# Building the expert-gate matrix from bf16 one-hots of eight tokens at a time instead of fp32 one-hots of four

## The chip, the cores and the metric

The kernel runs on one core of one Trainium2 chip. The metric is the device time of one execution in microseconds (us). The median of three runs of the kernel before is 3040.92 us (3037.68 to 3048.45). The engines are named as in the profile: PE is TensorE's matrix multiply and PEld its weight load, DVE is VectorE, ACT is ScalarE, POOL is GpSimd, SP is SyncE, which issues most DMA transfers.

## The reference

The program computes two transformer blocks over 512 tokens of 1024 features. The change sits in the last part, a PEER layer: each token picks 16 experts out of 16384 (= 128 x 128) for each of 8 heads, so 128 slots per token, each with an expert number (i, j) and a gate.

```python
best_s, best_c = lax.top_k(cand.reshape(T, PEER_HEADS, PEER_TOPK * PEER_TOPK), PEER_TOPK)
gates = jax.nn.softmax(best_s, axis=-1)
...
u = jnp.take(expert_u, ib, axis=0)
act = jax.nn.gelu(jnp.einsum('td,thkd->thk', xb, u).astype(jnp.float32))
w = (gb * act).astype(xb.dtype)
v = jnp.take(expert_v, ib, axis=0)
return jnp.einsum('thk,thkd->td', w, v)
```

## The kernel before

The last 128 tokens gather their experts' rows by indirect DMA (`gather_rows`). The first 384 tokens (NDENSE = 3 blocks of 128) do it densely: for every j of 128 the kernel multiplies all 384 tokens with the 128 experts (i, j) on TensorE (`expert_act`, L1397 to L1407: 24 matmuls of 384 columns), multiplies the result with the gates of (i, j) for each token (`expert_gate`), and multiplies that with the experts' output rows (`expert_out`).

For that the gates must stand in a dense matrix: for each token a 128 x 128 matrix over (i, j) that is zero except at its 128 slots. `gate_matrix` makes it. The slots of a token lie on the 128 partitions; `slots_T` has put i, j and the gate there with three transposes. For a token, a one-hot row of i for each slot, scaled with the slot's gate, and a one-hot row of j for each slot are built; their product on TensorE, summed over the slots, is the token's matrix. Both factors are fp32, and TensorE runs an fp32 product as two instructions.

The work goes in groups of four tokens, 96 groups in all. The letters of GATED say how a group is built. In an "A" group VectorE compares an iota row with i and with j in one instruction (L1382, 1024 elements), and ScalarE scales the one-hot of i with the gate, one instruction a token (L1384). In a "D" group VectorE compares j for four tokens (L1386, 512 elements) and builds the scaled one-hot of i itself, one instruction a token (L1388). TensorE makes the four products (L1391) into a PSUM tile `pg` of two buffers, and ScalarE copies it out into the staging tile `gstage` (L1393). Every 8 groups the staging tile of 2 MB goes to HBM as `gd` (L1395); it is read back later as `gread`.

`peer` (from L1430) sets the order: 15 expert products stand beside the retrieval, 4 after it, and then 21 (j from 19 to 39) are laid among the groups. Expert product j waits in the program's order for a group some 10 back (NLAG), and the last three (NLATE) follow the last group. A planner then orders each engine's instructions by a simulated timeline, with the groups at high priority; each engine runs its own list strictly in that order. For every expert product a weight tile of 512 KB is loaded and split into a high part by ScalarE (L245) and a low part by GpSimd (L248). After the groups comes the dense loop over 128 j.

The buffers are set by one line, `P.open(eg, "gate", "gstage 2; ohA 4; ohB 3")`: tile name and count. A new tile of a name waits until every reader of the tile that held its place is done.

Of the kernel before, what the change touches and what calls it, by code (L numbers as in the profile page):

```python
# [11 lines left out]
BF16 = mybir.dt.bfloat16  # L12
U32 = mybir.dt.uint32
AF = mybir.ActivationFunctionType
ALU = mybir.AluOpType
# [29 lines left out]
NDENSE = 3  # L45
NFIFO = 40
IN_ORDER = ((0, 0), (0, 1), (0, 2), (0, 3), (1, 0), (1, 1), (1, 2), (1, 3))
GATED = "ADADADAD"
NBESIDE = 15
NEARLY, NLATE, NLAG = 19, 3, 10  # L50
GATE_AHEAD = 8
# [118 lines left out]
class Prog:  # L170
# [1189 lines left out]
    def slots_T(self, i):  # L1360

        nc = self.nc
        p = self.b("pslT", [128, 3, 128])
        for w, a in enumerate((*self.sel, self.gate)):
            nc.tensor.transpose(p[:, w, :], a[:, i].rearrange("p a b -> p (a b)"), self.ident)
        t_ = self.B([128, 3, 128], f"slT{i}", 1)
        nc.scalar.activation(t_, p, AF.Copy)
        return t_

    def gate_matrix(self, slT, gd):  # L1370

        nc = self.nc
        for b in range(NDENSE * 4):
            st = self.b("gstage", [128, 128, 32])
            for q in range(8):
                p = self.b("pg", [128, 4, 128])
                t_ = b * 32 + q * 4
                sl, k = slT[t_ // 128], t_ % 128
                A4, one = self.b("ohA", [128, 4, 128]), self.b("ohB", [128, 2, 4, 128])
                iota = lambda n: self.iota[:, None, None, :].to_broadcast([128, n, 4, 128])  # L1380
                if GATED[q] == "A":
                    nc.vector.tensor_tensor(one, iota(2), sl[:, 0:2, k:k + 4, None].to_broadcast([128, 2, 4, 128]), op=ALU.is_equal)  # L1382
                    for r in range(4):
                        nc.scalar.activation(A4[:, r], one[:, 0, r], AF.Copy, scale=sl[:, 2, k + r:k + r + 1])  # L1384
                else:
                    nc.vector.tensor_tensor(one[:, 1:2], iota(1), sl[:, 1:2, k:k + 4, None].to_broadcast([128, 1, 4, 128]), op=ALU.is_equal)  # L1386
                    for r in range(4):
                        nc.vector.tensor_scalar(A4[:, r], self.iota, sl[:, 0, k + r:k + r + 1], sl[:, 2, k + r:k + r + 1],  # L1388
                                                op0=ALU.is_equal, op1=ALU.mult)
                for r in range(4):  # L1390
                    last = nc.tensor.matmul(p[:, r, :], A4[:, r], one[:, 1, r], start=True, stop=True)  # L1391
                self.gates_done.append(last.ins)
                nc.scalar.activation(st[:, :, q * 4:q * 4 + 4], p.rearrange("p t j -> p j t"), AF.Copy)  # L1393
                yield
            nc.sync.dma_start(gd[b], st.rearrange("p j t -> p (j t)"))  # L1395
# [141 lines left out]
def body(tc, I, out, dbg=None, manual=False):  # L1537
    nc = tc.nc
    with ExitStack() as es:
        if manual:  # L1540
            es.enter_context(tc.manual_schedule())
        P = Prog(tc, es, I, dbg)
# [83 lines left out]
        with ExitStack() as e1:  # L1626
# [5 lines left out]
            a = P.hgrn_in(0, U)  # L1632
            for h in range(8):
                b = P.hgrn_in(h + 1, U) if h < 7 else None
# [3 lines left out]
                a = b  # L1638
# [26 lines left out]
        eg = ExitStack()  # L1665

        def open_q2():
            eq1.close()
            P.open(eg, "gate", "gstage 2; ohA 4; ohB 3")

        def open_v():
            eg.close()
            P.qp = P.open(es, "peer2", "none 1")
        P.open_q2, P.open_v = open_q2, open_v
        P.peer(H4, gd, xd, row, out)

# [15 lines left out]
```

## Time and profile before

| | |
|---|---|
| median of 3 runs | 3040.92 us |
| profiled execution: its own time | 3040.9 us |
| span of its instructions | 3039.1 us |
| PE busy | 2938.0 us (97%), 15129 matmuls |
| DVE busy | 1867.7 us (61%) |
| ACT busy | 1245.4 us (41%) |
| POOL busy | 1352.4 us (44%) |
| mean granted TensorE clock | 0.989 of full speed |
| DMA over the span | 155 GB/s |

Busy time counts instructions from start to end. Matmuls overlap in TensorE's pipeline, so the distance between two starts, not their duration, says what one costs. The busy share over the whole span is a mean over stages with different limits; the groups' stage is some 180 us of it, from 1940 to 2120 us.

### The profile page before, as it was taken

Reading aid. Unit: us, or ns where it says so; the run is one execution under the profiler, and the core shown is the slowest. Engines: PE = TensorE matmul, PEld = TensorE weight load, DVE = VectorE, ACT = ScalarE, POOL = GpSimd, SP = SyncE. Lnnn points to the kernel's source line nnn. Section 1 sums busy time; section 2 is a strip of 40 time slices with the busy share of each in tenths; the row PEclk is TensorE's granted clock in tenths of the full one; section 3 lists DMA queues with packets and bytes.
Section 4 is the critical chain, followed back from the end, with each engine's and each line's share of the span. In section 5 each row is a group of like instructions: output and inputs, shape, how many; then the busy total and the mean of one; then the engine's idle time right before and its main releaser. Section 6 shows DMA issues by size and latency. Waiting matters only on the chain.

```text
span 3039.1 us, 40262 instructions
## 1 busy us (share of the span) xinstructions
PE 2938.0 (97%) x15129; PEld 2540.3 (84%) x15129; DVE 1867.7 (61%) x3017; ACT 1245.4 (41%) x2120; POOL 1352.4 (44%) x926
## 2 busy tenths in 40 slices
PE   7998998999999999999999999989999999999998
PEld 6877787888878887888888888888899999999887
DVE  4237664444133663355532489898678877777898
ACT  5455654222232453244432344576333333333333
POOL 3223213222234662233332344422677777777765
PEclk9998999999999999999999999999999999999999
DMA  4220003333332212322233432355988888898987
GB/s 155 63 63 15 1 30 103 97 97 97 97 107 88 63 46 73 108 83 81 82 105 114 130 97 88 125 190 195 303 299 296 311 312 302 289 324 300 320 321 264
DMA packets 174355, 473.60 MB, mean 156 GB/s; under 512 B 15057, under 2 KB 64593, under 8 KB 172625
## 3 DMA queue, kind: packets, MB, share of 16 engines
q1 hardware_dynamic: 137296, 336.80, 34.0%
q0 software_dynamic: 36864, 134.23, 12.5%
q8 instruction: 119, 1.95, 0.3%
q14 instruction: 76, 0.61, 0.1%
HBM read 439.49 MB, written 31.46 MB: 155 GB/s over the span
## 4 chain that ended last, share of the span: by engine, by line
PE 78%; issue 6%; DVE 5%; DMA 5%; ACT 3%; POOL 3%; SPq 0%; POOLq 0%; DVEq 0%; ACTq 0%
PE acc L271 15%; PE acc L272 15%; PE acc L273 15%; DMA urow<-ev,ei 3%; PE A L273 3%; PE A L272 3%; PE A L271 3%; PE B L272 3%; PE B L271 3%; PE B L273 3%; PE pg L1391 2%; PE i L810 2%; POOL urow L1339 1%; DMA rawx<-ev 1%; PE lev L987 1%
## 5 line engine op out<-in xcount | busy, mean ns | idle before, releaser
L248 POOL TENSOR_TENSOR lo<-raw,hi 128x1024 fp32r<-128x1024 f32 x224 | 558.1, 2493 | 946.3 <-ACT hi L245 920.5
L271 PE MATMUL acc<-u,hi 128*128 128x512 f32 (+3 forms) x2344 | 857.6, 367 | 4.0 <-DVE sil L912 1.5
L272 PE MATMUL acc<-u,hi 128*128 128x512 f32 (+3 forms) x2344 | 856.8, 366 | 0.2 <-DVE u L477 0.2
L273 PE MATMUL acc<-u,lo 128*128 128x512 f32 (+3 forms) x2344 | 856.9, 366 | 0.0
L245 ACT ACTIVATE hi<-raw 128x1024 fp32r<-128x1024 f32 x447 | 472.3, 1057 | 901.2 <-PE acc L272 457.4
L248 DVE TENSOR_TENSOR lo<-raw,hi 128x1024 fp32r<-128x1024 f32 x223 | 316.1, 1417 | 297.3 <-ACT hi L245 297.0
L271 PEld LDWEIGHTS acc<-u,hi 128*128 128x128 f32 (+1 forms) x2344 | 443.8, 190 | 59.0 <-issue 2.7
L272 PEld LDWEIGHTS acc<-u,hi 128*128 128x128 f32 (+1 forms) x2344 | 444.1, 189 | 54.7 <-issue 2.7
L273 PEld LDWEIGHTS acc<-u,lo 128*128 128x128 f32 (+1 forms) x2344 | 444.0, 189 | 48.7 <-issue 0.6
L1347 DVE SCALAR_TENSOR_TENSOR urow<-urow,h4row 128x1024 f32<-128x1024 f32 x128 | 200.8, 1575 | 94.5 <-DMA urow<-eu,ei 94.3
L1357 DVE SCALAR_TENSOR_TENSOR po<-urow,act,po 128x1024 f32<-128x1024 f32 x127 | 188.9, 1487 | 66.3 <-DMA urow<-ev,ei 65.4
L1339 POOL DMA_INDIRECT urow<-eu,ei x128 | 188.4, 1472 | 32.9 <-issue 21.4
L1417 ACT ACTIVATE wh<-wf 128x384 fp32r<-128x384 f32 x128 | 67.2, 526 | 312.4 <-PE D L272 246.4
L1339 POOL DMA_INDIRECT urow<-ev,ei x128 | 171.2, 1337 | 43.8 <-DVE po L1357 18.0
L248 POOL TENSOR_TENSOR lox<-rawx,hix 128x1024 fp32r<-128x1024 f32 x53 | 134.8, 2543 | 92.7 <-ACT hix L245 92.5
L1391 PE MATMUL pg<-ohB,ohA 128*128 128x128 f32 x768 | 105.1, 286 | 19.0 <-ACT gstage L1393 17.1
L1391 PEld LDWEIGHTS pg<-ohB,ohA 128*128 128x128 f32 x768 | 98.7, 197 | 24.4 <-ACT gstage L1393 20.9
L1418 DVE TENSOR_TENSOR wl<-wf,wh 128x384 fp32r<-128x384 f32 x128 | 98.8, 773 | 6.8 <-ACT wh L1417 5.1
L1384 ACT ACTIVATE ohA<-ohB,slT 128x128 f32<-128x128 f32 x192 | 61.4, 392 | 41.8 <-DVE ohB L1382 41.7
L1414 DVE TENSOR_TENSOR wf<-eact,gread 128x384 f32<-128x384 f32 x98 | 67.0, 684 | 17.0 <-DMA gread<-gd 15.9
L1388 DVE TENSOR_SCALAR ohA<-iota,slT 128x128 f32<-128x128 f32 x192 | 76.6, 461 | 0.0
L245 ACT ACTIVATE hix<-rawx 128x1024 fp32r<-128x1024 f32 x53 | 55.7, 1052 | 27.4 <-DMA rawx<-ev 27.4
(574 smaller groups left out, 5511.1 us busy)
## 6 DMA issues: line engine op xcount, KB each, us to landing
raw<-ut SPq DMA_DIRECT2D x128, 512.0 KB
raw<-ev SPq DMA_DIRECT2D x75, 512.0 KB
rawx<-ev SPq DMA_DIRECT2D x53, 512.0 KB
raw<-w_ret SPq DMA_DIRECT2D x48, 512.0 KB
gd<-gstage SPq DMA_DIRECT2D x12, 2048.0 KB
gread<-gd SPq DMA_DIRECT2D x32, 768.0 KB
raw<-w_gu SPq DMA_DIRECT2D x44, 512.0 KB
raw<-w_hg SPq DMA_DIRECT2D x32, 512.0 KB
```

Of the source, the lines that this page charges most:

```text
L245: self.nc.scalar.activation(hi, raw, AF.Copy)
L248: r = eng.tensor_tensor(lo, raw, hi.bitcast(F32), op=ALU.subtract)
L271: mm(out, a[0], b[0], start=start, stop=False)
L272: mm(out, a[0], b[1], start=False, stop=False)
L273: return mm(out, a[1], b[0], start=False, stop=stop).ins
L1339: r = nc.gpsimd.indirect_dma_start(out=u, out_offset=None, in_=src, in_offset=bass.IndirectOffsetOnAxis(ap=ei[:, s:s + 1], axis=0))
L1347: nc.vector.scalar_tensor_tensor(u, u, 1.0, row, op0=ALU.mult, op1=ALU.mult, accum_out=act[:, s:s + 1])
L1357: nc.vector.scalar_tensor_tensor(o, u, act[:, s:s + 1], o, op0=ALU.mult, op1=ALU.add)
L1388: nc.vector.tensor_scalar(A4[:, r], self.iota, sl[:, 0, k + r:k + r + 1], sl[:, 2, k + r:k + r + 1], op0=ALU.is_equal, op1=ALU.mult)
L1391: last = nc.tensor.matmul(p[:, r, :], A4[:, r], one[:, 1, r], start=True, stop=True)
L1417: nc.scalar.activation(wh, wf, AF.Copy)
L1418: nc.vector.tensor_tensor(wl, wf, wh.bitcast(F32), op=ALU.subtract)
```

## The change

The one-hots become bf16. VectorE builds both one-hots of eight tokens (two groups, called an octet below) in one comparison of 16 x 128 elements. To let it read 16-bit elements two by two, every i and j is first written twice side by side (`ij`), and the views are cut into pairs.

The gates stay exact: each fp32 gate is split into three bf16 parts that add up to it (`g3`, three ScalarE copies and two VectorE subtractions for 128 tokens). In two octets of three VectorE multiplies the one-hot of j with each of the three parts (three instructions of 8 x 128 elements), and TensorE makes each token's matrix with three bf16 products summed in PSUM. In every third octet ScalarE brings both one-hots back to fp32, group by group (one copy, four scaled copies), and TensorE multiplies in fp32 as before.

The PSUM tiles alternate between the names `psc` and `pg`, two buffers each, so four in place of two. `slots_T` writes i and j as bf16 and the gates as fp32 with two copies. The one-hot buffers are two of each name, each now holding an octet (or, for the fp32 operands, a group).

```diff
-GATED = "ADADADAD"
...
     def gate_matrix(self, slT, gd):
...
+        io = self.b("iotab", [128, 128], BF16)
+        nc.vector.tensor_copy(io, self.iota)
+        pairs = lambda a: a.rearrange("p n (c e) -> p n c e", e=2)
         for b in range(NDENSE * 4):
             st = self.b("gstage", [128, 128, 32])
+            if b % 4 == 0:
+
+                ij, g3 = self.b("ij", [128, 16, 2, 8, 2], BF16), self.b("g3", [128, 3, 128, 2], BF16)
+                ij_, g = slT[b // 4]
+                for w in range(2):
+                    nc.scalar.activation(ij[:, :, w], ij_[:, w].rearrange("p (n r) -> p n r", r=8)[:, :, :, None].to_broadcast([128, 16, 8, 2]), AF.Copy)
+                rest, r_ = self.b("grest", [128, 128]), g
+                for w in range(3):
+                    nc.scalar.activation(g3[:, w], r_[:, :, None].to_broadcast([128, 128, 2]), AF.Copy)
+                    if w < 2:
+                        nc.vector.tensor_tensor(rest, r_, g3[:, w, :, 0], op=ALU.subtract)
+                        r_ = rest
             for q in range(8):
...
-                if GATED[q] == "A":
-                    nc.vector.tensor_tensor(one, iota(2), sl[:, 0:2, k:k + 4, None].to_broadcast([128, 2, 4, 128]), op=ALU.is_equal)
+                k = b % 4 * 32 + q * 4
+                fp32 = (b * 4 + q // 2) % 3 == 2
+                if q % 2 == 0:
+                    one = self.b("ohA", [128, 16, 128], BF16)
+                    nc.vector.tensor_tensor(pairs(one), pairs(io[:, None, :].to_broadcast([128, 16, 128])),
+                                            ij[:, k // 8].rearrange("p w r e -> p (w r) e")[:, :, None, :].to_broadcast([128, 16, 64, 2]),
+                                            op=ALU.is_equal)
+                    if not fp32:
+                        gb = self.b("ohB", [128, 3, 8, 128], BF16)
+                        for w in range(3):
+                            nc.vector.tensor_tensor(pairs(gb[:, w]), pairs(one[:, 8:16]),
+                                                    g3[:, w, k:k + 8, None, :].to_broadcast([128, 8, 64, 2]), op=ALU.mult)
+                p = self.b("pg" if q % 2 else "psc", [128, 4, 128])
+                o = q % 2 * 4
+                if fp32:
+                    gb = self.b("ohB", [128, 2, 4, 128])
+                    nc.scalar.activation(gb[:, 0], one[:, o:o + 4], AF.Copy)
                     for r in range(4):
-                        nc.scalar.activation(A4[:, r], one[:, 0, r], AF.Copy, scale=sl[:, 2, k + r:k + r + 1])
+                        nc.scalar.activation(gb[:, 1, r], one[:, 8 + o + r], AF.Copy, scale=g[:, k + r:k + r + 1])
+                    for r in range(4):
+                        last = nc.tensor.matmul(p[:, r, :], gb[:, 0, r], gb[:, 1, r], start=True, stop=True)
                 else:
-                    nc.vector.tensor_tensor(one[:, 1:2], iota(1), sl[:, 1:2, k:k + 4, None].to_broadcast([128, 1, 4, 128]), op=ALU.is_equal)
                     for r in range(4):
-                        nc.vector.tensor_scalar(A4[:, r], self.iota, sl[:, 0, k + r:k + r + 1], sl[:, 2, k + r:k + r + 1],
-                                                op0=ALU.is_equal, op1=ALU.mult)
-                for r in range(4):
-                    last = nc.tensor.matmul(p[:, r, :], A4[:, r], one[:, 1, r], start=True, stop=True)
+                        for w in range(3):
+                            last = nc.tensor.matmul(p[:, r, :], one[:, o + r], gb[:, w, o + r], start=w == 0, stop=w == 2)
...
-            P.open(eg, "gate", "gstage 2; ohA 4; ohB 3")
+            P.open(eg, "gate", "gstage 2; iotab 1; ij 1; g3 1; grest 1; ohA 2; ohB 2")
```

## Rows read from the trace of the kernel before

**Rows 1.** Instructions of L1391, the groups' products: ns min/median/max, first and last start.

```profile
L1391 PE MATMUL pg<-ohB,ohA x768: 271/275/481, 1941.6 to 2119.8; 128*128 128x128 f32 x192
```

**Rows 2.** Busy time by stretch: us, then the engines, clock, DMA share, GB/s.

```profile
1940.00:2120.00 180.00, 160.89 (x1132) 155.48 (x1133) 165.65 (x285) 129.07 (x319) 40.24 (x16) 0.98 0.48 176
2200.00:2800.00 600.00, 600.00 (x3035) 546.40 (x3034) 469.23 (x510) 213.12 (x291) 437.19 (x249) 1.00 0.88 305
2860.00:3020.00 160.00, 158.43 (x701) 130.60 (x700) 150.81 (x140) 56.61 (x76) 112.44 (x64) 1.00 0.91 325
```

**Rows 3.** Groups of instructions by line, 1941 to 2121 us: count, busy us, mean ns, idle.

```profile
L1388 DVE TENSOR_SCALAR ohA<-iota,slT 128x128 f32<-128x128 f32 x192 | 76.6, 461 | 0.0
L1384 ACT ACTIVATE ohA<-ohB,slT 128x128 f32<-128x128 f32 x192 | 61.4, 392 | 41.8 <-DVE ohB L1382 41.7
L1382 DVE TENSOR_TENSOR ohB<-iota,slT 128x1024 f32<-128x1024 f32 x46 | 56.1, 1219 | 6.9 <-PE pg L1391 6.5
L1393 ACT ACTIVATE gstage<-pg 128x512 f32<-128x512 f32 x96 | 53.6, 585 | 8.6 <-PE pg L1391 8.2
L1386 DVE TENSOR_TENSOR ohB<-iota,slT 128x512 f32<-128x512 f32 x47 | 43.1, 917 | 6.1 <-ACT ohA L1384 3.6 <-PE pg L1391 1.2 <-issue 1.2
L271 PE MATMUL acc<-u,hi 128*128 128x384 f32 x123 | 43.1, 350 | 0.0
L248 POOL TENSOR_TENSOR lo<-raw,hi 128x1024 fp32r<-128x1024 f32 x16 | 40.8, 2552 | 125.2 <-ACT hi L245 125.2
L245 ACT ACTIVATE hi<-raw 128x1024 fp32r<-128x1024 f32 x15 | 15.8, 1053 | 0.0
```

**Rows 4.** Waits from 1936 to 2122 us: total us, times, longest.

```profile
ACT ohA L1384 <- DVE ohB L1382: 41.7, 28, 2.8
...
PE pg L1391 <- ACT gstage L1393: 17.1, 16, 1.8
```

**Rows 5.** Timeline of VectorE with GpSimd idle: start us, us, instruction.

```profile
2113.01 1.22 DVE L1382 TENSOR_TENSOR ohB<-iota,slT 128x1024 f32<-128x1024 f32 x1
2114.14 0.69 DVE L1386 TENSOR_TENSOR ohB<-iota,slT 128x512 f32<-128x512 f32 x1
2114.75 1.11 DVE L1388 TENSOR_SCALAR ohA<-iota,slT 128x128 f32<-128x128 f32 x4
2115.77 1.22 DVE L1382 TENSOR_TENSOR ohB<-iota,slT 128x1024 f32<-128x1024 f32 x1
```

**Rows 6.** Timeline of GpSimd and VectorE around one weight split.

```profile
1967.16 2.88 POOL L248 TENSOR_TENSOR lo<-raw,hi 128x1024 fp32r<-128x1024 f32 x1 [8.12 <-ACT hi L245]
...
1967.71 2.87 DVE L1386 TENSOR_TENSOR ohB<-iota,slT 128x512 f32<-128x512 f32 x1
```

**Rows 7.** Timeline of PE: two groups' products; two expert matmuls, twelve apart.

```profile
2099.17 1.95 PE L1391 MATMUL pg<-ohB,ohA 128*128 128x128 f32 x16
...
2126.16 0.34 PE L271 MATMUL acc<-u,hi 128*128 128x384 f32 x1
...
2128.24 0.34 PE L271 MATMUL acc<-u,hi 128*128 128x384 f32 x1
```

**Rows 8.** Timeline of PE: 128-column matmuls of one instruction each (retention layer).

```profile
1509.37 0.27 PE L271 MATMUL s<-qk 128*128 128x128 f32 x1
1509.49 0.27 PE L272 MATMUL s<-qk 128*128 128x128 f32 x1
1509.60 0.28 PE L273 MATMUL s<-qk 128*128 128x128 f32 x1
```

**Rows 9.** Weight loads: of those matmuls, and the program's only bf16 ones.

```profile
L271 PEld LDWEIGHTS s<-qk x32: 187/188/193, 1266.6 to 1509.3; 128*128 128x128 f32 x32
...
L620 PEld LDWEIGHTS <-identb x32: 95/96/151, 66.4 to 181.3; 128*128 128x128 bf16 x32
```

**Rows 10.** ScalarE copies from SBUF of 512 and 256 elements, elsewhere in the program.

```profile
L322 ACT ACTIVATE qk<-ra 128x512 fp32r<-128x512 f32 x16 | 10.0, 628 | 10.8 <-POOL ra L1099 10.4
...
L886 ACT ACTIVATE lnsq<-lnd 128x256 f32<-128x256 f32 x8 | 3.3, 411 | 1.8 <-DVE lnd L884 1.8
```

More of the change, by code (lines that the diff above doesn't have):

```diff
@@ L1365, in slots_T @@
             nc.tensor.transpose(p[:, w, :], a[:, i].rearrange("p a b -> p (a b)"), self.ident)
-        t_ = self.B([128, 3, 128], f"slT{i}", 1)
-        nc.scalar.activation(t_, p, AF.Copy)
-        return t_
+        ij, g = self.B([128, 2, 128], f"ijT{i}", 1, BF16), self.B([128, 128], f"gT{i}", 1)
+        nc.scalar.activation(ij, p[:, 0:2], AF.Copy)
+        nc.scalar.activation(g, p[:, 2], AF.Copy)
+        return ij, g
     def gate_matrix(self, slT, gd):
         nc = self.nc
+        io = self.b("iotab", [128, 128], BF16)
@@ L1373, in gate_matrix @@
+        nc.vector.tensor_copy(io, self.iota)
+        pairs = lambda a: a.rearrange("p n (c e) -> p n c e", e=2)
         for b in range(NDENSE * 4):
             st = self.b("gstage", [128, 128, 32])
-            for q in range(8):
[L1376 to L1380, printed above, removed]
-                if GATED[q] == "A":
-                    nc.vector.tensor_tensor(one, iota(2), sl[:, 0:2, k:k + 4, None].to_broadcast([128, 2, 4, 128]), op=ALU.is_equal)
+            if b % 4 == 0:
[9 more added lines that the diff above has]
+                        r_ = rest
+            for q in range(8):
+                k = b % 4 * 32 + q * 4
[15 more added lines that the diff above has]
+                    nc.scalar.activation(gb[:, 0], one[:, o:o + 4], AF.Copy)
```

## The prediction

> **What bounds the kernel now.** I first placed the groups' stage: its products run from 1941.6 to 2119.8 us [rows 1]. Next I compared the stretches [rows 2]. From 2200 to 2800 us PE is busy all 600 us, and from 2860 to 3020 us 158.43 of 160, so the dense loop behind the stage runs at TensorE's pace and starts when the stage ends. In the stage DMA is busy 0.48, in the loop 0.88; the loop's loads start with the loop and move with it. So I count a microsecond won or lost in the stage as one at the end. The profiled execution took 3040.9 us beside a span of 3039.1, equal to the median of the runs, 3040.92; sums below are made against it.
>
> Inside the stage the fullest engine is VectorE: 165.65 us busy of 180 [rows 2]. Its own work is less. With GpSimd idle, one period of two groups steps from 2113.01 to 2114.14 (1.13 us for the comparison of 1024 elements), to 2114.75 (0.61 for that of 512), to 2115.77 (1.02 for four scaled one-hots): 2.76 us [rows 5], times 48 periods 132.5 us. Where a weight split runs on GpSimd, VectorE's instruction lasts with it: the 512-element comparison took 2.87 us in place of 0.69 beside a split of 2.88 [rows 5, 6]. There are 16 splits of 2.55 us [rows 3], 40.8 us, and 165.65 less 132.5 says that some 33 us of them fell on VectorE. The other 14 of the 180 us it waits. TensorE needs less: two groups' 16 instructions take 1.95 us less a last one of 0.28, over 15 steps, 0.11 us each [rows 1, 7], so 768 make 85.5 us; the expert matmuls step by 2.08/12 = 0.173 us [rows 7], and some 367 of them (123 from one of three lines [rows 3]) make 63.5: 149 of 180. ScalarE is busy 129 us [rows 2], and it is often early: it waits 41.7 us for VectorE's comparisons [rows 4].
>
> **The change, part by part.** *VectorE.* The new comparison covers 2048 bf16 elements an octet. If two 16-bit elements pass per step, that is the 1024 steps of the old one, 1.13 us; a multiplication of 1024 bf16 elements is 512 steps, 0.605 us [rows 5]. 48 x 1.13 + 32 x 3 x 0.605 = 54.4 + 58.1 = 112.5 us in place of 132.5: 20 us less. If each element takes a step, the slope of those two rows (0.52 us for 512 elements) makes 2.17 and 1.13 us, 104 + 108 = 212 us. No bf16 instruction with two tensors ran before, so both ends stay. I take the first: both operands and the output are 16-bit and laid in pairs.
> [...]
>
> *GpSimd's splits* are untouched, 33 us of VectorE. All new VectorE instructions have two SBUF tensors, like the one held up in [rows 6], so I keep 33.
>
> *TensorE.* A third of the groups stays fp32: 32 x 8 x 0.11 = 28.5 us. The other 64 have 12 bf16 products each, 768 in place of 512 instructions. By the expert matmuls 128 columns stream in 0.173/3 = 0.058 us [rows 7]. But single 128-column matmuls with 4-byte weights step by 0.11 us [rows 8], twice that, so there the weight load sets the pace. The bf16 loads last 96 ns where the others last 188 [rows 9], about half. So 0.058 us is the low end and 0.11 the high; by the load's ratio I take 0.06: 46 us. The stage's sum is 46 + 28.5 + 63.5 = 138 us. At 0.11 it is 84.5 + 28.5 + 63.5 = 176.5.
> [...]
>
> *ScalarE* loses 192 scaled copies (61.4 us) and gains 128 of 0.392 (50.2), 32 copies of 512 elements at 0.628 (20.1) and 15 small ones that prepare pairs and parts at 0.41 (6.2) [rows 3, 10]: 129 + 15 = 144 us. The 96 copies out of PSUM stay.
>
> *Starts and end.* For each 128 tokens `ij` and `g3` have one buffer, and three copies with two subtractions between make a chain of about 2 us (an estimate: three times 0.41 [rows 10] and two short subtractions) before VectorE can multiply. The comparison beside it hides about half of the three: 4 us, plus 2 at the first for the pair copies of 0.41 each [rows 10] and the cast. The last octet is fp32 and ends with ScalarE's two groups, 2 x 1.8 us, where the old one ended with VectorE: 3 us. Together 9 (bounds 4 and 15). No DMA is added or moved past another queue; the 12 writes of `gd` come at the stage's pace.
>
> *Waits.* The 17.1 us that TensorE waits for ScalarE's copies out of `pg` [rows 4] should nearly go with four PSUM tiles. What is late next is the one-hot buffer. An fp32 octet takes both places of `ohB`, and the next octet's multiplications wait until its first group has been copied by ScalarE (0.628 + 0.392 + three further ones at some 0.3, about 1.8 us), then multiplied, PE ending some 0.3 behind. So per three octets the chain is comparison 1.13, fp32 group 2.1, multiplications 1.82, comparison 1.13, multiplications 1.82: 8.0 us where VectorE's own work is 3 x 1.13 + 6 x 0.605 = 7.0. That is 1 us of wait in each of 16 cycles, 16 us, and it replaces the present 14. Behind the waiting multiplication stand VectorE's next comparison and with it all engines. If no wait shows, 0; if ScalarE's PSUM copies (0.585) and weight rounding (1.053) [rows 3] also stand ahead of each fp32 group, and expert matmuls ahead of its products, up to 2 us a cycle, 32.
>
> Sum for the 180 us: 112.5 + 33 + 9 + 16 = 170.5, 9.5 us less, 3040.9 - 9.5 = **3031 us**. With waits of 0 and starts of 4 it is 149.5, 3010; with 32 and 15 it is 192.5, 3053.
>
> **Rivals.** *The buffers eat the gain.* VectorE's 20 us are given back as waits for ScalarE and TensorE, which now stand in a two-place loop with it. For it: all three would be at 138 to 146 us of work (VectorE 112.5 + 33), close together, in strict order. Against it: ScalarE today waits more than it is waited for [rows 4]. It turns to a loss when waits and starts exceed 34.5 us. With 32 + 9 it gives 186.5: 3047 us.
> *TensorE becomes the bound, the side of a loss.* If a bf16 product costs 0.11 us, 176.5 us of products plus the 14 us of unfilled time of today make 190: 3051 us. It decides from about 0.10 us a product. Speaking for it is [rows 8], against it [rows 9]. [...]
> *VectorE does not read pairs.* 212 + 33 + 9 + some 6 of waits = 260 us: 3121 us. The pairs are then worthless. Against it is only the layout; nothing in the trace shows it.
>
> **How the numbers follow.** A run of this kernel tells about 0.3%, 9 us, from no change. The forecast case (pairs read, a light product, waits of 0 to 20 us, 3010 to 3036) has 0.50; of it 0.43 lies more than 9 us below and 0.07 within. The buffers have 0.27 (3036 to 3053): 0.16 within 9 us, 0.11 slower. TensorE as the bound has 0.13: 0.03 within, 0.10 slower. One element a step has 0.10, all slower. So faster 0.43, same 0.26, slower 0.31. The range 3010 to 3062 leaves out the last case alone, its high end some way above the 3051 of the second-last; the forecast's own range is 3010 to 3036.
>
> **What would show it.** In the changed profile: the comparison of 2048 elements at about 1.2 us and the multiplications at about 0.69 (2.2 and 1.2 if no pairs are read); bf16 products that step by about 0.06 us; TensorE's wait for the copies out of PSUM nearly gone; VectorE waiting for TensorE ahead of the multiplication behind each fp32 octet, about 1 us a cycle; the last product near 2110 us; and the loop's pace of 3035 matmuls in 600 us [rows 2] unchanged, so that the end moves by as much as the stage does. Wrong would make it: a planner's order that puts expert matmuls in front of groups that are ready, bf16 instructions that GpSimd holds up longer than before, or a loop whose start waits for a late `gread`.

## The result and the profile after

The changed kernel takes 3064.95 us (median of 4 runs, 3064.63 to 3072.39), the kernel before beside it 3041.9 us: a ratio of 1.008, 95% interval 1.0056 to 1.0104. It is slower by 0.8%; the forecast was 3031 us, range 3010 to 3062.

Nearly all of it lies in the groups' stage. The instructions of the groups' products in the changed kernel (ns min/median/max, first and last start):

```profile
L1416 PE MATMUL psc<-ohB,ohA x384: 216/219/330, 1941.2 to 2136.5; 128*128 128x128 bf16 x192
...
L1412 PE MATMUL pg<-ohB x128: 272/275/582, 1950.1 to 2141.8; 128*128 128x128 f32 x128
```

They run from 1941.2 to 2141.8 us, 200.6 us where the kernel before had 178.2 [rows 1]. That is 22.4 us of the 24.1 by which the span grew (3063.2 and 3039.1). Busy time by stretch, with the columns of [rows 2], shows the same from both sides:

```profile
1940.00:2140.00 200.00, 163.47 (x1376) 152.07 (x1375) 142.57 (x149) 129.21 (x293) 39.42 (x15) 0.89 0.41 158
2200.00:2800.00 600.00, 600.00 (x3034) 546.15 (x3033) 464.19 (x516) 211.76 (x289) 437.74 (x249) 1.00 0.87 305
```

The dense loop runs as before, 3034 matmuls in 600 us. In the stage VectorE is busy 142.57 us where it was 165.65, so its work did shrink, by 23 us. But it idles 57.4 of 200 us (200 - 142.57) where it idled 14.35 of 180. TensorE's granted clock in the stage fell from 0.98 to 0.89 of full speed. The groups of instructions (count, busy us, mean ns, idle ahead and what ended it):

```profile
L1402 DVE TENSOR_TENSOR ohB<-ohA,g 128x1024 bf16<-128x1024 bf16 x96 | 78.1, 869 | 13.7 <-PE psc L1412 6.4 <-PE pg L1412 3.4 <-PE pg L1416 1.8
L1396 DVE TENSOR_TENSOR ohA<-iotab,ij 128x2048 bf16<-128x2048 bf16 x48 | 65.9, 1376 | 45.9 <-PE pg L1416 27.5 <-ACT ij L1384 8.8 <-ACT ohB L1410 8.2
```

In [rows 3] VectorE idled 6.9 and 6.1 us ahead of its comparisons. Now it idles 45.9 us there, 27.5 of them until TensorE is done with products of `pg`, which are the last readers of an octet's place of `ohA`, and 8.2 until ScalarE has copied from such a place. And the waits of the stage (total us, times, longest) show that TensorE waits for VectorE in turn, while its old wait for the copies out of PSUM, 17.1 us in [rows 4], is down to 1.3:

```profile
PE psc L1416 <- DVE ohB L1402: 30.1, 29, 4.1
...
DVE ohA L1396 <- PE pg L1416: 27.5, 17, 4.7
```

Two places in the timeline show how the two engines come to wait for each other. At the first, VectorE's rows come first, then those of TensorE:

```profile
2056.54 1.90 DVE L1402 TENSOR_TENSOR ohB<-ohA,g 128x1024 bf16<-128x1024 bf16 x3
2058.36 1.22 DVE L1396 TENSOR_TENSOR ohA<-iotab,ij 128x2048 bf16<-128x2048 bf16 x1
2059.68 1.90 DVE L1402 TENSOR_TENSOR ohB<-ohA,g 128x1024 bf16<-128x1024 bf16 x3
2064.54 2.57 DVE L1396 TENSOR_TENSOR ohA<-iotab,ij 128x2048 bf16<-128x2048 bf16 x2 [2.96 <-PE pg L1416]
```

```profile
2057.29 0.22 PE L1416 MATMUL psc<-ohB,ohA 128*128 128x128 bf16 x1 [2.15 <-DVE ohB L1402]
...
2058.14 0.42 PE L270 MATMUL acc<-u,hi 128*128 128x384 f32 x1
...
2059.00 0.52 PE L271 MATMUL acc<-u,hi 128*128 128x384 f32 x1
2059.32 0.52 PE L272 MATMUL acc<-u,lo 128*128 128x384 f32 x1
...
2062.93 0.33 PE L270 MATMUL acc<-u,hi 128*128 128x384 f32 x1
2063.10 0.73 PE L1416 MATMUL psc<-ohB,ohA 128*128 128x128 bf16 x10
2063.67 0.83 PE L1416 MATMUL pg<-ohB,ohA 128*128 128x128 bf16 x12
```

TensorE has waited 2.15 us for the first of VectorE's three multiplications, which end at 2058.44 (2056.54 + 1.90). But its list then holds 19 expert matmuls, from 2058.14 on, and the rest of the octet's products starts at 2063.10, 4.7 us late. VectorE has written the next octet by 2061.58. Its comparison after that needs the place of `ohA` that those products read, and waits 2.96 us.

The second place is a wait for `ohB`. First ScalarE and VectorE, then TensorE alone:

```profile
2068.09 1.27 ACT L1410 ACTIVATE ohB<-ohA,gT 128x128 f32<-128x128 bf16 x4
2068.24 1.90 DVE L1402 TENSOR_TENSOR ohB<-ohA,g 128x1024 bf16<-128x1024 bf16 x3 [1.13 <-PE psc L1412]
...
2070.05 1.22 DVE L1396 TENSOR_TENSOR ohA<-iotab,ij 128x2048 bf16<-128x2048 bf16 x1
...
2072.97 2.28 DVE L1402 TENSOR_TENSOR ohB<-ohA,g 128x1024 bf16<-128x1024 bf16 x3 [1.70 <-PE pg L1412]
```

```profile
2067.96 0.42 PE L270 MATMUL acc<-u,hi 128*128 128x384 f32 x1
...
2071.71 0.33 PE L270 MATMUL acc<-u,hi 128*128 128x384 f32 x1
2071.88 1.05 PE L1412 MATMUL pg<-ohB 128*128 128x128 f32 x8
```

ScalarE has the second fp32 group of an octet ready at 2069.36 (2068.09 + 1.27). TensorE's list holds expert matmuls from 2067.96 on (22 of them), so the group's product starts at 2071.88, 2.5 us late. VectorE's next multiplication needs that place of `ohB` and waits until 2072.97, and the comparison behind it in VectorE's list comes later too.

### The profile page after: what moved, and what is told of

Its sections match the earlier page's. It is cut to its first block, busy times and chain, and to the rows that moved or that the text cites. A ratio compares the mean times of both kernels' runs of the same rounds, so it can differ in the third digit from the quotient of the medians.

```text
span 3063.2 us, 40514 instructions
## 1 busy us (share of the span) xinstructions
PE 2939.0 (96%) x15385; PEld 2534.2 (83%) x15385; DVE 1845.0 (60%) x2880; ACT 1249.4 (41%) x2106; POOL 1347.6 (44%) x926
## 4 chain that ended last, share of the span: by engine, by line
PE 86%; DVE 7%; issue 3%; ACT 2%; DMA 1%; POOL 1%; SPq 0%; DVEq 0%; POOLq 0%; ACTq 0%
PE acc L270 16%; PE acc L271 16%; PE acc L272 16%; PE A L272 3%; PE A L271 3%; PE A L270 3%; PE B L271 3%; PE B L270 3%; PE B L272 3%; PE i L809 2%; DVE ohB L1402 1%; PE lev L986 1%; PE C L272 1%; PE C L271 1%; PE C L270 1%
## 5 line engine op out<-in xcount | busy, mean ns | idle before, releaser
L247 DVE TENSOR_TENSOR lo<-raw,hi 128x1024 fp32r<-128x1024 f32 x223 | 303.4, 1361 | 297.3 <-ACT hi L244 296.9
L1439 DVE TENSOR_TENSOR wf<-eact,gread 128x384 f32<-128x384 f32 x98 | 86.2, 881 | 22.1 <-DMA rawx<-ev 21.0
L1396 DVE TENSOR_TENSOR ohA<-iotab,ij 128x2048 bf16<-128x2048 bf16 x48 | 65.9, 1376 | 45.9 <-PE pg L1416 27.5
L1416 PEld LDWEIGHTS <-ohA 128*128 128x128 bf16 x768 | 55.2, 110 | 41.3 <-issue 28.6
L1402 DVE TENSOR_TENSOR ohB<-ohA,g 128x1024 bf16<-128x1024 bf16 x96 | 78.1, 869 | 13.7 <-PE psc L1412 6.4
L1416 PE MATMUL psc<-ohB,ohA 128*128 128x128 bf16 x384 | 40.8, 243 | 31.5 <-DVE ohB L1402 30.1
```

Source lines behind the costliest of these rows:

```text
L247: r = eng.tensor_tensor(lo, raw, hi.bitcast(F32), op=ALU.subtract)
L1402: nc.vector.tensor_tensor(pairs(gb[:, w]), pairs(one[:, 8:16]), g3[:, w, k:k + 8, None, :].to_broadcast([128, 8, 64, 2]), op=ALU.mult)
L1416: last = nc.tensor.matmul(p[:, r, :], one[:, o + r], gb[:, w, o + r], start=w == 0, stop=w == 2)
L1439: nc.vector.tensor_tensor(wf.rearrange("p (b t) -> p b t", t=32), a.rearrange("p (b t) -> p b t", t=32), gr[:, :, j % 4, :], op=ALU.mult)
```

## The experiments

Twelve kernels ran. The ratios stand against runs of the kernel before on the same chip; its medians lay between 3040.4 and 3042.2 us. An edit also makes the planner order the lists anew, so a difference of a few us is not read here.

**Four PSUM tiles alone**, in the kernel before.

```diff
-                p = self.b("pg", [128, 4, 128])
+                p = self.b("pg" if q % 2 else "psc", [128, 4, 128])
```

> The kernel before, with the groups' products going to four PSUM tiles (psc and pg in turn) in place of two; nothing else. It shows what this part of the change gives alone. VectorE paces the stage before (132.5 us of own work and 33 us beside GpSimd of 180), so most of TensorE's 17.1 us of waits for the copies out of PSUM were not on the path: I expect 0 to 5 us less than before, 3036 to 3041. If those waits are on the path, 10 to 15 us less.

Measured: 3051.45 us, ratio 1.0027 (1.0016 to 1.0039), a small loss where nothing or a small gain was expected. VectorE's waits for `psc` products came up (13.8 us ahead of L1386), and TensorE's granted clock from 1940 to 2100 us was 0.93 where the kernel before had 0.99. Why was not settled. At any rate this part of the change gives the kernel before nothing.

**Two places for each one-hot tile**, in the kernel before.

```diff
-            P.open(eg, "gate", "gstage 2; ohA 4; ohB 3")
+            P.open(eg, "gate", "gstage 2; ohA 2; ohB 2")
```

> The kernel before with two places for each one-hot tile (ohA 2; ohB 2) in place of four and three. First theory (the one-hot buffers: VectorE must wait until TensorE is done with a place two back, so any lateness on TensorE or ScalarE comes back to VectorE): 8 to 20 us slower than before, with VectorE's waits for pg products in the stage grown from some 8 us to 20 or more. Rival (the expert matmuls' place in TensorE's list is what makes the changed kernel slow): within 5 us of before.

Measured: 3133.15 us, ratio 1.0299 (1.0254 to 1.0343). The sign was expected, not the size: over four times the upper figure. VectorE's idle time ahead of L1382, over the same 48 instructions, first in the kernel before and then here:

```profile
L1382 DVE TENSOR_TENSOR ohB<-iota,slT 128x1024 f32<-128x1024 f32 x48 | 60.0, 1251 | 8.1 <-PE pg L1391 6.5 <-ACT slT L1367 1.1
```

```profile
L1382 DVE TENSOR_TENSOR ohB<-iota,slT 128x1024 f32<-128x1024 f32 x48 | 79.1, 1648 | 90.5 <-PE pg L1391 89.3 <-ACT slT L1367 1.1
```

So at two places the stage is paced by the round from VectorE over TensorE back to VectorE, in fp32 too. Two places hold eight tokens here, half of what two octets hold, so the run does not price the changed kernel's two places.

**One-hot tiles by group**, in the changed kernel: the same room, cut into four places of ohA and three of ohB, each for four tokens.

```diff
...
-                if q % 2 == 0:
-                    one = self.b("ohA", [128, 16, 128], BF16)
...
+                one = self.b("ohA", [128, 8, 128], BF16)
...
-                        gb = self.b("ohB", [128, 3, 8, 128], BF16)
+                    gb = self.b("ohB", [128, 3, 4, 128], BF16)
...
-            P.open(eg, "gate", "gstage 2; iotab 1; ij 1; g3 1; grest 1; ohA 2; ohB 2")
+            P.open(eg, "gate", "gstage 2; iotab 1; ij 1; g3 1; grest 1; ohA 4; ohB 3")
```

> The changed kernel with one-hot tiles of one group of four tokens in place of an octet, four of ohA and three of ohB in the same room, so that a place comes free after one group; VectorE pays for it with twice as many instructions, some 10 us more of its own work (48 x 0.08 + 96 x 0.07). First theory (buffers): the waits of VectorE for TensorE shrink by more than that, 5 to 20 us less than the changed kernel, 3045 to 3060. Rival (TensorE's list): no gain, 3065 to 3078.

Measured: 3035.01 us, ratio 0.9974 (0.996 to 0.9988): 30 us less than the changed kernel, more than expected, and less than the kernel before. The last product starts at 2110.0 us. VectorE's work grew from 144.0 to 155.8 us (80.8 and 75.0), and its idle time ahead of comparisons and multiplications fell from 59.6 to 24.1 us:

```profile
L1401 DVE TENSOR_TENSOR ohB<-ohA,g 128x512 bf16<-128x512 bf16 x192 | 80.8, 478 | 6.9 <-PE pg L1411 4.5 <-PE pg L1415 0.8 <-PE psc L1415 0.6
L1395 DVE TENSOR_TENSOR ohA<-iotab,ij 128x1024 bf16<-128x1024 bf16 x96 | 75.0, 809 | 17.2 <-ACT ij L1384 6.8 <-ACT ohB L1409 4.4 <-PE pg L1415 4.2
```

**All octets in bf16**, in the changed kernel.

```diff
-                fp32 = (b * 4 + q // 2) % 3 == 2
+                fp32 = False
```

> The changed kernel with every octet in bf16: ScalarE brings nothing back to fp32. VectorE's own work grows from 112.5 to 48 x 1.13 + 144 x 0.605 = 141 us, TensorE's products come to 96 x 12 x 0.056 = 65 us. If the loop through ScalarE in every third octet is what holds VectorE up, its waits nearly go and the stage is 141 + 33 + some 10: 10 us less than the changed kernel, near 3055. If TensorE's list and the two places are the reason, VectorE waits as long as before beside more own work: 3075 to 3090.

Measured: 3061.14 us, ratio 1.0061 (1.0037 to 1.0086), some 4 us less than the changed kernel, between the two expectations. VectorE waits less, but 17.9 us ahead of its comparisons are still for `pg`, with no fp32 octet left.

```profile
L1402 DVE TENSOR_TENSOR ohB<-ohA,g 128x1024 bf16<-128x1024 bf16 x144 | 105.8, 790 | 1.2
L1396 DVE TENSOR_TENSOR ohA<-iotab,ij 128x2048 bf16<-128x2048 bf16 x48 | 73.4, 1535 | 25.7 <-PE pg L1416 17.9 <-ACT ij L1384 5.5 <-PE psc L1416 2.3
```

The waits ahead of the multiplications (13.7 us before this edit) are gone with the fp32 octets; those ahead of the comparisons are not. So ScalarE's loop is one cause and not the only one. How large it is this run does not tell: VectorE's own work grew from 144.0 to 179.2 us, and its waits fell from 59.6 to 26.9, as they might on a fuller engine for any reason.

**Only ohA by group**, and **only ohB by group**, in the changed kernel.

```diff
...
-                    one = self.b("ohA", [128, 16, 128], BF16)
+                one = self.b("ohA", [128, 8, 128], BF16)
...
-            P.open(eg, "gate", "gstage 2; iotab 1; ij 1; g3 1; grest 1; ohA 2; ohB 2")
+            P.open(eg, "gate", "gstage 2; iotab 1; ij 1; g3 1; grest 1; ohA 4; ohB 2")
```

> The changed kernel with only the comparisons and their tile ohA by group of four tokens (four places in the same room); the multiplied one-hots ohB stay in octets, two places, though written by six instructions. VectorE waited 45.9 us ahead of its comparisons in the changed kernel, most of it for TensorE, and 13.7 ahead of the multiplications. If the places of ohA are what counts, it takes most of what the kernel with both by group gained (30 us): 3037 to 3046. If those of ohB count, 3055 to 3068.

```diff
...
-                        gb = self.b("ohB", [128, 3, 8, 128], BF16)
+                    gb = self.b("ohB", [128, 3, 4, 128], BF16)
...
-            P.open(eg, "gate", "gstage 2; iotab 1; ij 1; g3 1; grest 1; ohA 2; ohB 2")
+            P.open(eg, "gate", "gstage 2; iotab 1; ij 1; g3 1; grest 1; ohA 2; ohB 3")
```

> The changed kernel with only the multiplied one-hots ohB by group, three places; the comparison and its tile ohA stay in octets, two places. If the places of ohA are what counts, it stays slow, 3055 to 3068; if those of ohB count, 3037 to 3046.

Measured: with ohA by group 3048.46 us, ratio 1.0031 (1.0019 to 1.0043); with ohB alone 3066.08 us, 1.0092 (1.0075 to 1.0109). So ohB's places alone give nothing, ohA's give some 16 us, about half of the 30, a little short of what was expected; the rest comes only with both. These are net figures, since smaller instructions cost VectorE time (0.61 us for 512 fp32 elements beside 1.13 for 1024 in [rows 5]): with ohA by group its waits fell from 59.6 to 33.4 us and its work rose from 144.0 to 158.5; with ohB by group they went to 50.4 and 150.8.

**A third place for the octet tile ohA.** To make room for it, both kernels of this pair make three expert products fewer ahead of the loop.

```diff
-NFIFO = 40
+NFIFO = 37
...
-            P.open(eg, "gate", "gstage 2; iotab 1; ij 1; g3 1; grest 1; ohA 2; ohB 2")
+            P.open(eg, "gate", "gstage 2; iotab 1; ij 1; g3 1; grest 1; ohA 3; ohB 2")
```

(The last two lines are in the second kernel alone.)

> The changed kernel with 37 in place of 40 expert products made ahead of the dense loop (NFIFO 37; 18 in place of 21 among and behind the groups). It only makes room for the next run and is its control. Either theory: the products moved into the loop cost there what they cost here, so 3060 to 3070, as the changed kernel; up to 15 us less if fewer expert matmuls among the groups take waits away that were more than their own time.

> The same with a third place for the octet tile ohA; every instruction is otherwise the same. If the two places of ohA are what hold VectorE, 12 to 30 us less than with two (NFIFO 37), with VectorE's waits ahead of its comparisons down from some 40 us to below 20. If the size of the octet's instructions or TensorE's list is the reason and the places are not, within 5 us of it.

Measured: two places 3068.09 us, ratio 1.0093 (1.0076 to 1.011); three places 3051.98 us, 1.0042 (1.0028 to 1.0057): 16 us less, with the same instructions in the same sizes. First two places, then three:

```profile
L1396 DVE TENSOR_TENSOR ohA<-iotab,ij 128x2048 bf16<-128x2048 bf16 x48 | 65.6, 1372 | 37.9 <-PE pg L1416 20.5 <-ACT ohB L1410 9.2 <-ACT ij L1384 6.5
```

```profile
L1396 DVE TENSOR_TENSOR ohA<-iotab,ij 128x2048 bf16<-128x2048 bf16 x48 | 59.7, 1255 | 23.6 <-PE pg L1416 13.3 <-ACT ij L1384 4.6 <-ACT ohB L1410 4.4
```

The gain is where it was expected; the waits fell to 23.6 and not below 20. TensorE's granted clock from 1940 to 2100 us rose with it, from 0.89 to 0.93.

**No expert products among the groups**, in the changed kernel. It ran once, so there is no interval.

```diff
-            done = min((j - NEARLY) * ng // m, ng)
+            done = ng
```

> The changed kernel with none of the 21 expert products among the groups: all follow the last group, so TensorE has nothing but the groups' products in the stage and GpSimd no weight splits. If VectorE's waits come from expert matmuls that stand ahead of ready products in TensorE's list, its 27.5 us of waits for pg fall below 8 and the stage from the first to the last product is some 130 to 140 us (200 in the changed kernel). If the loop of ScalarE and the two places alone holds VectorE, at least 16 us of waits stay and the stage is over 150 us. The whole time is 3060 to 3090 either way, since some 75 us of expert matmuls now stand behind the stage.

Measured: 3080.49 us in all, as expected; the stage's products run from 1933.0 to 2081.6 us, 149 us, between what the two theories said.

```profile
L1402 DVE TENSOR_TENSOR ohB<-ohA,g 128x1024 bf16<-128x1024 bf16 x96 | 60.8, 686 | 22.9 <-PE psc L1412 21.5
L1396 DVE TENSOR_TENSOR ohA<-iotab,ij 128x2048 bf16<-128x2048 bf16 x48 | 58.5, 1220 | 8.9 <-PE pg L1416 6.0 <-ACT ij L1384 2.8
```

Both theories have a share. The comparisons' wait for `pg` falls from 27.5 to 6.0 us, so most of that one comes with the expert products. The edit also takes their weight splits off GpSimd and their rounding off ScalarE (the mean comparison is 1.22 us here, 1.38 in the changed kernel), so the run alone does not part these from the matmuls in TensorE's list; the rows from 2056.54 on show the list at work. The multiplications' wait for the fp32 products rises from 9.8 to 21.5 us: that is the loop through ScalarE, some 1.5 us at a time, as in these rows:

```profile
2004.03 0.68 ACT L1410 ACTIVATE ohB<-ohA,gT 128x128 f32<-128x128 bf16 x2
2004.47 0.78 PE L1412 MATMUL psc<-ohB 128*128 128x128 f32 x4 [0.94 <-ACT ohB L1410]
...
2005.09 0.69 ACT L1410 ACTIVATE ohB<-ohA,gT 128x128 f32<-128x128 bf16 x2
2005.54 0.78 PE L1412 MATMUL psc<-ohB 128*128 128x128 f32 x4 [0.28 <-ACT ohB L1410]
...
2006.36 1.90 DVE L1402 TENSOR_TENSOR ohB<-ohA,g 128x1024 bf16<-128x1024 bf16 x3 [1.55 <-PE psc L1412]
```

**Two PSUM tiles**, in the kernel by group.

```diff
-                p = self.b("pg" if q % 2 else "psc", [128, 4, 128])
+                p = self.b("pg", [128, 4, 128])
```

> The kernel with both one-hot tiles by group, with all products in two PSUM tiles as before the change in place of four. Four tiles alone made the kernel before 0.27% slower. If that holds here too, 2 to 10 us less than with four, near 3028; if TensorE now waits for ScalarE's copies out of PSUM as it did before the change (17.1 us), 5 to 15 us more, near 3045.

Measured: 3061.89 us, ratio 1.0069 (1.005 to 1.0088), 27 us more than with four: the second expectation, and more than it said. TensorE waits for ScalarE's copies again, 24.1 us in all, 16.4 of them ahead of the fp32 products:

```profile
PE pg L1411 <- ACT gstage L1417: 16.4, 9, 3.3
...
PE pg L1415 <- ACT gstage L1417: 7.7, 8, 2.5
```

So four tiles, worth nothing to the kernel before, are needed by this one.

**NLAG 4 in place of 10**, in the changed kernel and in the one by group.

```diff
-NEARLY, NLATE, NLAG = 19, 3, 10
+NEARLY, NLATE, NLAG = 19, 3, 4
```

> The changed kernel with NLAG 4 in place of 10: an expert product may stand in the lists only behind the group 4 back, so fewer expert matmuls come early. If expert matmuls ahead of ready products make TensorE late, VectorE's waits for pg shrink and it is 5 to 20 us less, 3045 to 3060. If the two places hold it whatever the list, 3060 to 3070. If TensorE then lacks matmuls to fill with, more, up to 3080.

> The kernel with both one-hot tiles by group and NLAG 4. With finer places TensorE's lateness matters less, so the theory of the places says within 6 us of NLAG 10, 3029 to 3041; the theory of TensorE's list says 5 to 15 us less.

Measured: 3061.9 us, ratio 1.008 (1.0062 to 1.0098), the changed kernel's own ratio; and 3037.35 us, 0.999 (0.9977 to 1.0003), 2 us from the kernel by group. Both are what was expected if the places hold VectorE whatever the list; its wait for `pg` ahead of comparisons is still 22.3 us in the first. So where this bound lies hardly matters. That does not settle how a better list would do, since the planner still places the matmuls behind it freely.

## Why the prediction was wrong

*What held.* The comparison of 2048 bf16 elements took the time that 1024 fp32 elements take in [rows 5], 1.22 us and not some 2.2, and three multiplications of 1024 took 1.90, in the rows of the stage without experts. The prediction's choice of the first of its two values was the author's estimate; no row of the kernel before showed it. No kernel here compares bf16 elements that are not laid in pairs, so what the pairs add was not shown. The sum 112.5 + 33 us forecast 145.5 of VectorE's work; 144.0 were measured (78.1 and 65.9). The bf16 products are light: two groups of twelve start 0.67 us apart, 0.056 us a product.

```profile
2064.34 0.83 PE L1416 MATMUL psc<-ohB,ohA 128*128 128x128 bf16 x12
...
2065.01 0.83 PE L1416 MATMUL pg<-ohB,ohA 128*128 128x128 bf16 x12
```

Each of these products has a weight load of its own, and the loads keep the step: the 46 loads of the 46 products from 2063.10 on end 2.57 us after the first starts, though one lasts 98 ns (median):

```profile
2063.10 2.57 PEld L1416 LDWEIGHTS <-ohA 128*128 128x128 bf16 x46 [0.16 <-issue]
```

At 0.056 us the groups in bf16 take 43 us (768 x 0.056, an estimate from these rows), where the prediction took 46. So the rivals "TensorE becomes the bound" (0.11 us a product) and "VectorE does not read pairs" are out. TensorE's wait for PSUM copies went (from 17.1 us to 1.3), and the loop behind the stage passed the stage's loss on.

*What failed* is the term "waits", 16 us with bounds of 0 and 32. VectorE idles 57.4 us of 200, starts included, where 16 + 9 stood in the sum. The step worked out one round only, VectorE to ScalarE to TensorE and back over `ohB`, and took TensorE as ready whenever an operand was. That round came out about as sized: 13.7 us ahead of the multiplications, and 21.5 where nothing else stands in TensorE's list, against the 16 predicted. The starts did too (8.8 us of waits for `ij`). What the step put at nothing is the wait on `ohA`: 27.5 us for TensorE and 8.2 for ScalarE, 35.7 in all. With two places for octets, VectorE cannot start a comparison until TensorE is done with the octet two back, and TensorE's list has expert matmuls ahead of it. The runs show this three ways: a third place takes 16 us away, finer places of `ohA` 16, and with no expert products the wait for `pg` falls from 27.5 to 6.0 us. Expert matmuls ahead of a product were named in the bound, at the fp32 group, but together with ScalarE's other work they were priced at 1 us a cycle; a planner's order that does this stood among the signs of being wrong, without a price.

The rival "the buffers eat the gain" (0.27, 3047 us) was the right kind and too small by 18 us. The trace of before gave the warning too: it ran with four and three places for single groups, and [rows 3] showed waits of 13 us under that depth. The prediction let its 16 us take the place of these waits and gave no reason why those on the comparison's tile should go. In tokens the room did not shrink: comparisons had three places of four tokens (`ohB` in the kernel before) and now have two of eight, scaled one-hots had four of four and now two of eight, or of four in an fp32 octet. What went are the places beyond the one that VectorE writes and the one that TensorE reads. With two there is none left, so that TensorE's lateness comes straight back. That way of counting is an argument, but all runs on the places fit it: giving back spare places of `ohA` (a third octet, or four groups) gains 16 us, a spare place of `ohB` alone nothing, both 30.

*Left open.* How much of the 22 us is TensorE's lower clock. The lower level is half of the full one (0.50 in the last section's rows), so a granted clock of 0.89 over 200 us means some 44 us at the lower level; 0.98 over 180 us in the kernel before means 7. TensorE loses at most half of that, 22 us against 4 (estimates from these rows): a bound as large as the loss. Waits and clock came together here. In the rows from 2056.54 on TensorE waits for VectorE, then its clock falls, and ten expert matmuls (2059.00 to 2062.20) that step 0.32 us in place of 0.173 make up some 1.5 of the 2.96 us that VectorE waits next (an estimate). The runs with more places have the higher clock too (from 1940 to 2100 us 0.97 by group, 0.88 in the changed kernel), so what they gain may be partly the clock; no run here parts the two. And why four PSUM tiles cost the kernel before 0.27%.

## What to carry to other kernels

When a tile is made larger and its places fewer, do not count only what they hold: count, before and after, the places left beyond the one being written and the one being read, and ask what may stand in front of the consumer in its engine's list. A lighter instruction on the fullest engine was worth here only what the round over its buffers let it use: VectorE's busy time fell from 165.65 to 142.57 us, its idle time rose from 14.35 to 57.4. The bf16 one-hots pay only once their places are cut to groups, and then little: 3035 us, 0.9974 of the kernel before (0.996 to 0.9988).

## What the runs showed of the hardware

TensorE's granted clock in the changed kernel's stage shows two levels, 0.50 and 1.00 of full speed: of the 200 stretches of 1 us from 1940 to 2140 us, 148 stand at 1.00, 35 at 0.50 and 17 between. Stretches of 20 us are a mixture, 0.80 to 1.00. The first row is the lowest of the last. The second is the lower level, over the expert matmuls shown above, and the third the full clock behind them:

```profile
2040.00:2060.00 20.00, 15.63 (x106) 14.62 (x107) 14.11 (x14) 12.09 (x28) 4.77 (x2) 0.80 0.41 158
...
2058.90:2062.10 3.20, 3.20 (x12) 3.20 (x11) 2.57 (x4) 0.12 (x1) 0.00 (x0) 0.50 0.00 0
2062.30:2065.00 2.70, 2.70 (x40) 2.54 (x39) 0.46 (x1) 1.06 (x2) 0.00 (x0) 1.00 0.02 6
```

At 0.50 a matmul of 384 columns lasts 0.52 us and steps by 0.32; at full clock it lasts 0.33 to 0.34 and steps by some 0.17. Before the fall TensorE had waited 2.15 us for VectorE.

A VectorE instruction that reads what the one before it wrote started later here than one that doesn't. In the stage without experts a comparison of 1.22 us is followed by its own multiplication 1.32 us after its start (1998.99); behind another, of an octet that has no multiplications, comes one of the octet before, 1.13 us after its start (1983.49), the step from a comparison of the same length to an independent instruction in [rows 5]. In the changed kernel it is 1.32 us from a comparison to its own multiplication (2058.36 to 2059.68) and 1.15 to an instruction that reads other tiles (2006.97 to 2008.12). The rows of the stage without experts:

```profile
1983.49 1.21 DVE L1396 TENSOR_TENSOR ohA<-iotab,ij 128x2048 bf16<-128x2048 bf16 x1
1984.62 0.68 DVE L1402 TENSOR_TENSOR ohB<-ohA,g 128x1024 bf16<-128x1024 bf16 x1
...
1998.99 1.22 DVE L1396 TENSOR_TENSOR ohA<-iotab,ij 128x2048 bf16<-128x2048 bf16 x1
...
2000.31 1.90 DVE L1402 TENSOR_TENSOR ohB<-ohA,g 128x1024 bf16<-128x1024 bf16 x3
```
